# Modulation steps of two and four weight blocks, and a weight ring of seven raw and four split buffers

## The chip, the cores and the metric

The kernel runs on one core of a Trainium2 chip. The metric is the time of one execution on the device, in microseconds (us); a kernel's time is the median of three runs. TensorE (PE in the profile) multiplies, ScalarE (ACT) and VectorE (DVE) prepare operands and empty the accumulators, GpSimd (POOL) helps them, and SyncE (SP) does nothing but issue transfers, one after the other, from its queue.

## The reference, cut to what matters

One decoder layer in float32, for a prompt of 256 tokens and 8 sequences of 4 sampled tokens, so 288 token columns in all. The modulation `mod = silu(c) @ w_ada + b_ada` has 9 rows (one prompt, eight sequences) and 6 x 2048 columns, which are split into shift, scale and gate of two sub-layers.

```
sh1, sc1, gt1, sh2, sc2, gt2 = split(mod, 6)
u   = rms_norm(x) * (1 + sc1) + sh1
mix = token_mixers(u, ...)          # w_in, gated delta rule, causal pooling, w_proj_a/b, w_out
x   = x + gt1 * mix
h   = rms_norm(x) * (1 + sc2) + sh2
x   = x + gt2 * ((silu(gate) * up) @ w_down),   gate, up = split(h @ w_gate_up, 2)
```

The weights, some 360 MB, are read once each. `w_ada` alone is 2048 x 12288 numbers, 100 MB of them.

## The kernel before, in words

**The large products.** `gemm` (line 129) makes a panel of 512 output columns in four accumulators of PSUM. It goes through the contraction in groups of KB = 2 blocks of 128 rows. For each group `load_split` (line 117) loads a raw weight tile of 128 x 1024 float32 (512 KB), and for each of its two blocks ScalarE casts a high half `wh` (line 123) and VectorE, now and then GpSimd, subtracts it to get a low half `wl` (line 124). A group is 24 products on TensorE (line 141): four accumulators, two blocks, and the three terms high x high, high x low, low x high. There are 472 groups: 208 in the mixer (numbers 0 to 207 here, in the order of the program) and 264 in the feed-forward part (208 to 471).

**The buffers.** Raw tiles stand in a ring of RAW = 5, high halves in a ring of WH = 6 and low halves in another of 6, which is three groups of two. A tile is loaded or written when the tile that had its place is no longer needed: a raw tile when its low halves are made, a split tile when TensorE has used it for the last time. A raw tile and two pairs of split tiles take the same room per partition, so that two of the one can be had for two less of each of the other kind.

**The modulation.** `ada` (line 184) computes columns of `mod` straight from raw float32 weights, without a split: four products (eight records in a trace) with the 32-column tile of the conditioning, for each block of 128 rows of `w_ada`. It is a generator. Each step loads the blocks of `pair` steps of the contraction, does their products, and yields. `Fill` advances it between groups of the large products: after each group it adds `every` to a count, and takes a step for each whole number. In the order of the program there are these generators:

- `first_ada`, shift and scale of the first norm, in five pieces (`STEPS`) for 2, 2, 4, 4 and 4 blocks of the hidden size. Each must be done before the first large product with these blocks, since their normed input is scaled by it. Their raw tiles stand in a ring of 4 of their own (pool `st`).
- `later`, gate of the first and scale and shift of the second sub-layer, during the rest of the mixer. Each block of rows takes two raw tiles (`per` = 2), and these stand in the ring of RAW that the large products use.
- `last_ada`, gate of the second sub-layer, from the last of the mixer into the feed-forward part, also in that ring.

**The order.** A scheduler places each engine's instructions beforehand, from the program's order, from priorities and from its own estimate of times; on the chip each engine then works through its list strictly in order, and waits where an operand or a buffer isn't free. SyncE's list holds all loads of weights. At the start of the feed-forward part it also holds a load of the final norm's gain (`fg`, line 1036), whose place is that of tiles that VectorE (line 1028) needs until the second norm is done. The pooling branch loads its own small weights `pw` (line 850) through the same list.

Of the kernel before, what the change touches and what calls it, by code (L numbers as in the profile page):

```python
# [22 lines left out]
H = 8  # L23
DFF = 5632
KB = 2
RAW, WH = 5, 6
NQ = 21
EPS = 1e-6

# [1 line left out]
M_SH1, M_SC1, M_GT1, M_SH2, M_SC2, M_GT2 = 0, 16, 32, 48, 64, 80  # L31
# [42 lines left out]
def tile_step(ctx: ExitStack, tc: tile.TileContext, at, t):  # L74
# [21 lines left out]
    def bc(ap, axis, shape):  # L96
        return ap.unsqueeze(axis).broadcast_to(shape)

    def in_turn(ins):

        tc.stamp_issue_order_token(ins.ins, "modulation")


    def load_raw(srcs, pool=None, kbs=KB):
        n = KB * 512
        if pool is None:
            raw = wpool.tile([P, n], F32, tag="raw", name="raw", bufs=RAW)
        elif pool is qp:
            raw = fquad("raw").rearrange("p k n -> p (k n)")[:, 0:n]
        else:  # L110
            raw = pool.tile([P, n], F32, tag="raw", name="raw", bufs=4)
        raw = raw.rearrange("p (k n) -> p k n", k=kbs)
        for ap, lo, hi in srcs:
            dma(out=raw[:, :, lo:hi], in_=ap.rearrange("(k p) n -> p k n", p=P))  # L114
        return raw
# [11 lines left out]
    def gemm(srcs_of, xs, evac, kbs, eng=vec, late=False):  # L127


        ps = [psg.tile([P, 512], F32, tag="g", name=f"g{j}") for j in range(4)]  # L130
        kbs = list(kbs)
        for c in range(0, len(kbs), KB):
            wh, wl = load_split(srcs_of(kbs[c]), eng)
            for j in range(4):
                o = ps[j][:, 0:N]
                last = c + KB == len(kbs)
                terms = [(w, x, i) for i in range(KB) for w, x in ((wh, 0), (wh, 1), (wl, 0))]
                if late and c == 0:
                    terms.sort(key=lambda v: v[1])
                for n, (w, x, i) in enumerate(terms):  # L140
                    pe.matmul(o, w[i][:, j * P:(j + 1) * P], xs(kbs[c + i])[x], start=c + n == 0,  # L141
                              stop=last and n == 3 * KB - 1)
                if last:
                    with tc.high_priority():
                        evac(j, o)
            fill()

    def cols_of(w, c0):
        return lambda kb: [(w[kb * P:(kb + KB) * P, c0:c0 + 512], 0, 512)]
# [30 lines left out]
    def ada(*d0s, n=16, pool=None):  # L180

        m = n * len(d0s)
        w = m // 4 * P
        ps = psd.tile([P, 512], F32, tag="ada", name="ada")
        per = max(m // 8, 1)
        step = max(8 // m, 1)
        pair = 2 if m == 8 else 1
        for c in range(0, 16, step * pair):
            loads = []
            for k in range(c, c + step * pair, step):  # L190
                raws = []
                for x in range(per):
                    if per > 1:
                        d = (d0s if len(d0s) > 1 else (d0s[0], d0s[0] + 8))[x]
                        srcs = [(t["w_ada"][0, k * P:(k + 1) * P, d * P:(d + 8) * P], 0, 1024)]
                    else:
                        srcs = [(t["w_ada"][0, k * P:(k + step) * P, d0 * P:(d0 + n) * P], i * n * P, (i + 1) * n * P)
                                for i, d0 in enumerate(d0s)]
                    raws.append(load_raw(srcs, qp if pool and d0s[0] == M_SH1 and k >= 8 else pool, step))
                loads.append((k, raws))  # L200

            todo = [(k, raws, i, j) for k, raws in reversed(loads) for i in range(step) for j in (2, 3, 0, 1)]
            for y, (k, raws, i, j) in enumerate(todo):
                x, q = divmod(j, 4 // per)
                with tc.high_priority() if y else nullcontext():
                    in_turn(pe.matmul(ps[32 * j:32 * j + 32, 0:w], cpad[:, k + i, :], raws[x][:, i, q * w:(q + 1) * w],  # L206
                                      start=c == 0 and y < 4, stop=c + step * pair == 16 and y + 4 >= len(todo)))
            if c + step * pair < 16:
                yield
        sb = wpool.tile([P, 512], F32, tag="adasb", name="adasb", bufs=1)  # L210
        act.copy(sb[:, 0:w], ps[:, 0:w])
        for i in range(0, w, P):
            pe.transpose(ps[:, i:i + P], sb[:, i:i + P], ident)
        pv = ps[:, 0:w].rearrange("p (b q m) -> p q b m", q=4, m=32)
        k = 4 // len(d0s)
        for i, d0 in enumerate(d0s):
            md = mod[:, d0:d0 + n, :].rearrange("p (q b) m -> p q b m", q=k)
            v = va[:, d0:d0 + n].rearrange("p (q b) -> p q b", q=k)
            vec.tensor_tensor(md, pv[:, i * k:(i + 1) * k, :, 0:9], bc(v, 3, [P, k, n // k, 9]), ALU.add)
        yield  # L220
# [19 lines left out]
    fill = Fill()  # L240
# [4 lines left out]
    FIRST = (C_Q, C_XP, C_K, C_XP + 512, C_V, C_Z, C_GB, C_GB + 512, C_GB + 1024)  # L245
    STEPS = ((0, 2), (2, 4), (4, 8), (8, 12), (12, 16))
    later = chain(*(ada(d) for d in (M_GT1, M_SC2, M_SH2)))
    last_ada = ada(M_GT2)

    def first_ada(k0, k1, pool):  # L250
        return ada(M_SH1 + k0, M_SC1 + k0, n=k1 - k0, pool=pool)
# [54 lines left out]
    with tc.tile_pool(name="st", bufs=1) as st:  # L306
# [68 lines left out]
        for n, (k0, k1) in enumerate(STEPS):  # L375
            dn = k1 - k0
# [23 lines left out]
            if n == 1:  # L400

                for p in range(2):
                    pst = aux("pst")
                    for h in range(3):
# [3 lines left out]
                        for j in range(4):  # L408
                            m = 24 * (4 * h + j)
# [3 lines left out]

            more = n + 1 < len(STEPS)
            fill.gen = first_ada(*STEPS[n + 1], st) if more else later
            fill.every = 8 / (dn // KB * len(FIRST) - 5) if more else 0.4
            for p, c0 in enumerate(FIRST):
                def evac(j, ps, n=n, p=p):
                    a = acc[p][:, j, :]
# [544 lines left out]
    for p in range(4):  # L964
# [31 lines left out]
            for k in range(3):  # L996
                scaled_samples(k)
        gemm(cols_of(t["w_out"][0], 512 * p), xs_m, evac, range(16))
    fill.gen, fill.every, fill.n = last_ada, 0.15, 5


    rn = cst.tile([P, 3], F32, name="rn")
# [124 lines left out]
```

## Time and profile before

| | |
|---|---|
| median of 3 runs | 1842.74 us (1838.03 to 1844.19) |
| the profiled execution | 1836.14 us, span of its instructions 1834.4 us |
| granted clock of TensorE | 0.991 over the span |
| busy: TensorE, VectorE, ScalarE, GpSimd | 97%, 54%, 41%, 11% |
| read from HBM | 361.16 MB, 201 GB/s over the span |

A row of the page's groups gives line, engine, operation, out<-in by the program's names, and after the bar the busy time, the mean time of one in ns, and the idle time before. Products are pipelined, so the duration of one (some 0.29 us) is longer than the step from one to the next; the steps between starts are what counts. A granted clock of 1.00 is 2.4 GHz and 0.50 is 1.2 GHz, and nothing between occurs in this trace.

### The profile page before, as it was taken

The page shows a single profiled execution, that of the slowest core. Times are in us where ns is not written, and L with a number is a line of the kernel's source. Part 1 is how long each engine was busy: PE and PEld are TensorE (multiplying, and loading weights), DVE is VectorE, ACT ScalarE, POOL GpSimd, SP SyncE. Part 2 cuts the span into 40 slices and gives each one's busy share as a digit, 9 for nine tenths or more (in the row PEclk, how much of TensorE's full clock was granted, in tenths as well). Part 3 has the DMA queues.
Part 4 walks back from the last instruction along what each step waited for, and adds up shares of the span by engine and source line. Part 5 has one row for each costly group of instructions (what it writes and reads, how often), then busy time and mean ns, then how long its engine had stood idle before and what let it go on. Part 6 is the DMA issues. An engine that isn't in the chain of part 4 may idle for free.

```text
span 1834.4 us, 37797 instructions
## 1 busy us (share of the span) xinstructions
PE 1785.7 (97%) x14778; PEld 1657.4 (90%) x14778; DVE 986.2 (54%) x2126; ACT 746.4 (41%) x1522; POOL 206.7 (11%) x376
## 2 busy tenths in 40 slices
PE   5999999999999999999998999999999999999997
PEld 4889998878988787889988999999999999999997
DVE  2466579665645665565555444454444454444454
ACT  4533356433444232344443443443333444444333
POOL 1000025340102232211142000000000000000000
PEclk9999999999999999999999999999999999999999
DMA  9898766666676584876566766655555555555552
GB/s 305 289 322 276 227 204 199 211 213 201 213 244 219 170 253 162 264 255 199 175 217 202 218 198 195 213 181 166 165 168 163 170 163 163 164 169 163 161 160 98
DMA packets 227210, 371.23 MB, mean 202 GB/s; under 512 B 18335, under 2 KB 118168, under 8 KB 226608
## 3 DMA queue, kind: packets, MB, share of 16 engines
q1 hardware_dynamic: 223224, 357.02, 61.0%
q0 software_dynamic: 3808, 11.80, 2.1%
q8 instruction: 116, 1.90, 0.4%
q14 instruction: 62, 0.51, 0.1%
HBM read 361.16 MB, written 7.96 MB: 201 GB/s over the span
## 4 chain that ended last, share of the span: by engine, by line
PE 86%; DMA 6%; DVE 5%; ACT 1%; issue 1%; SPq 0%; POOL 0%; POOLq 0%; ACTq 0%; DVEq 0%
PE g L141 76%; PE ada L206 4%; DMA raw<-in_w_in_dram 3%; DMA raw<-in_w_ada_dram 2%; DVE cy L274 1%; DVE wl L124 1%; PE pss L746 1%; DVE rq L1028 1%; ACT wh L123 1%; PE pks L700 1%; PE py L872 0%; SPq L114 0%; PE py L631 0%; PE pp L636 0%; DMA pw<-in_pool_w_dram 0%
## 5 line engine op out<-in xcount | busy, mean ns | idle before, releaser
L141 PE MATMUL g<-rq,wh 128*128 128x288 f32 x7296 | 1493.2, 299 | 10.3 <-ACT wh L123 4.0
L141 PEld LDWEIGHTS g<-rq,wh 128*128 128x128 f32 x7296 | 1172.9, 188 | 64.4 <-issue 22.7
L141 PE MATMUL g<-rq,wl 128*128 128x288 f32 x3648 | 1075.2, 296 | 0.7 <-POOL wl L124 0.7
L124 DVE TENSOR_TENSOR wl<-raw,wh 128x512 fp32r<-128x512 f32 x910 | 598.8, 692 | 661.4 <-ACT wh L123 659.8
L123 ACT CAST wh<-raw 128x512 fp32r<-128x512 f32 x944 | 543.9, 618 | 878.5 <-PE g L141 630.3
L141 PEld LDWEIGHTS g<-rq,wl 128*128 128x128 f32 x3648 | 687.6, 189 | 7.4 <-issue 4.5
L206 PE MATMUL ada<-raw,cpad 128*32 128x512 f32 (+2 forms) x1152 | 106.6, 473 | 15.3 <-DMA raw<-in_w_ada_dram 14.9
L168 POOL TENSOR_TENSOR ro<-ro,cfix 128x1 f32<-128x1 f32 (+1 forms) x3 | 1.7, 557 | 844.1 <-DVE ro L1091 844.1
L423 DVE TENSOR_TENSOR acc<-acc,g 128x288 f32<-128x288 f32 x144 | 62.2, 449 | 22.7 <-PE g L141 22.4
L206 PEld LDWEIGHTS ada<-raw,cpad 128*32 128x32 f32 x1152 | 28.0, 113 | 39.3 <-issue 19.4
L124 POOL TENSOR_TENSOR wl<-raw,wh 128x512 fp32r<-128x512 f32 x34 | 46.6, 1393 | 45.7 <-ACT wh L123 45.4
L141 PE MATMUL g<-q,wh 128*128 128x288 f32 x256 | 51.0, 294 | 0.0
L274 DVE SCALAR_TENSOR_TENSOR cy<-xc,vb,cy 128x312 f32<-128x312 f32 x72 | 43.6, 623 | 5.3 <-ACT cy L272 4.7
L141 PEld LDWEIGHTS g<-q,wh 128*128 128x128 f32 x256 | 41.3, 189 | 0.0
L141 PE MATMUL g<-q,wl 128*128 128x288 f32 x128 | 37.9, 296 | 0.0
L935 DVE SCALAR_TENSOR_TENSOR x<-g,mod,x 128x256 f32<-128x256 f32 x48 | 23.0, 480 | 12.5 <-PE g L141 11.5
L1061 DVE TENSOR_TENSOR fgg<-fgg,g 128x288 f32<-128x288 f32 x44 | 20.0, 454 | 10.9 <-PE g L141 8.7
L141 PEld LDWEIGHTS g<-q,wl 128*128 128x128 f32 x128 | 24.0, 188 | 0.0
L749 DVE SCALAR_TENSOR_TENSOR sst<-sst,cds,pss 128x128 f32<-128x128 f32 x64 | 18.1, 343 | 7.9 <-PE pss L746 7.7
L1056 DVE SCALAR_TENSOR_TENSOR fgg<-fth,fgg 128x288 f32<-128x288 f32 x44 | 20.0, 455 | 3.9 <-ACT fgg L1055 1.3
L1054 ACT ACTIVATE fth<-g 128x288 f32<-128x288 f32 x44 | 18.1, 412 | 7.3 <-PE g L141 5.4
L644 POOL MEMSET T<- 32x64 f32 x8 | 1.1, 142 | 168.5 <-PE pab L432 151.0
(324 smaller groups left out, 948.4 us busy)
## 6 DMA issues: line engine op xcount, KB each, us to landing
raw<-in_w_gate_up_dram SPq DMA_DIRECT2D x352, 256.0 KB, 3.1
raw<-in_w_in_dram SPq DMA_DIRECT2D x144, 512.0 KB, 5.3
raw<-in_w_ada_dram SPq DMA_DIRECT2D x128, 512.0 KB, 4.4
raw<-in_w_down_dram SPq DMA_DIRECT2D x88, 512.0 KB, 3.8
raw<-in_w_ada_dram SPq DMA_DIRECT2D x128, 256.0 KB, 5.5
raw<-in_w_out_dram SPq DMA_DIRECT2D x32, 512.0 KB, 3.7
raw<-in_w_proj_b_dram SPq DMA_DIRECT2D x16, 512.0 KB, 4.6
raw<-in_w_proj_a_dram SPq DMA_DIRECT2D x16, 512.0 KB, 5.0
```

What stands on the lines that cost most here:

```text
L123: act.copy(wh[i], raw[:, i, :])
L124: eng.tensor_tensor(wl[i], raw[:, i, :], wh[i].bitcast(F32), ALU.subtract)
L141: pe.matmul(o, w[i][:, j * P:(j + 1) * P], xs(kbs[c + i])[x], start=c + n == 0, stop=last and n == 3 * KB - 1)
L206: in_turn(pe.matmul(ps[32 * j:32 * j + 32, 0:w], cpad[:, k + i, :], raws[x][:, i, q * w:(q + 1) * w], start=c == 0 and y < 4, stop=c + ste ...
L274: vec.scalar_tensor_tensor(y[:, 0:L], xc[:, m:m + L], vb[:, 24 * m + no:24 * m + no + 1], y[:, 0:L], ALU.mult, ALU.add)
L423: vec.tensor_tensor(a, a, ps, ALU.add)
L700: pe.matmul(pks[NS * i:NS * i + NS, x * P:(x + 1) * P], km[i // 2][:, i % 2, b, :], S[i][:, b, :], start=b == 0, stop=b == NB - 1)
L746: pe.matmul(pss, kt[r, 0, :], wx[b0 // 4][r].rearrange("p b v -> p (b v)"), start=True, stop=True)
L935: vec.scalar_tensor_tensor(x[:, j, 0:NP], ps[:, 0:NP], mod[:, gate + d, 0:1], x[:, j, 0:NP], ALU.mult, ALU.add)
L1028: vec.scalar_tensor_tensor(b[:, d, 0:NP], hp, mod[:, M_SH2 + k, 0:1], a[:, d, 0:NP].bitcast(F32), ALU.add, ALU.subtract)
L1056: vec.scalar_tensor_tensor(gg, th, 1.0, gg, ALU.add, ALU.mult)
L1061: vec.tensor_tensor(gg, gg, ps, ALU.mult)
```

## The change

Two constants and three rates change. RAW goes from 5 to 7 and WH from 6 to 4. `pair` is now chosen by `m`, the number of output blocks: the pieces with 4 blocks in shift and scale each (m = 8) take four blocks of rows at a time instead of two, the full-width ones of `later` and `last_ada` (m = 16) two instead of one, and the second piece with 2 (m = 4) two steps instead of one; the very first piece stays as it was. `every` is halved, or nearly so, to go with it.

```
-RAW, WH = 5, 6
+RAW, WH = 7, 4
...
-        pair = 2 if m == 8 else 1
+        pair = {4: 1 if d0s[0] == M_SH1 else 2, 8: 4, 16: 2}[m]
...
-            fill.every = 8 / (dn // KB * len(FIRST) - 5) if more else 0.4
+            fill.every = 4 / (dn // KB * len(FIRST) - 5) if more else 0.2
...
-    fill.gen, fill.every, fill.n = last_ada, 0.15, 5
+    fill.gen, fill.every, fill.n = last_ada, 0.08, 2
```

In the built order TensorE stops for the modulation (a run of line 206 between other instructions) at 96 places before and at 52 now. Three places follow.

TensorE, end of the second and start of the third piece's panels (`g_1309` to `g_1312` are the accumulators of group 17, `g_1362` to `g_1365` those of group 18; line 213 turns the finished modulation for group 18's input). Before:

```order
L141 MATMUL g_1311<-rq,wl 128x288
L206 MATMUL ada<-raw,cpad 32x256 x8
L141 MATMUL g_1312<-rq,wh 128x288 x2
L141 MATMUL g_1312<-rq,wl 128x288
L141 MATMUL g_1312<-rq,wh 128x288 x2
L141 MATMUL g_1312<-rq,wl 128x288
L432 MATMUL pab<-xn_271,wab 32x288 x4
L141 MATMUL g_1362<-rq,wh 128x288
L141 MATMUL g_1363<-rq,wh 128x288
L141 MATMUL g_1364<-rq,wh 128x288
L206 MATMUL ada<-raw,cpad 32x256 x8
```

And now:

```order
L213 MATMUL ada<-cfix,adasb 128x128 x2
L141 MATMUL g_1311<-rq,wl 128x288
L141 MATMUL g_1312<-rq,wh 128x288 x2
L141 MATMUL g_1312<-rq,wl 128x288
L141 MATMUL g_1312<-rq,wh 128x288 x2
L141 MATMUL g_1312<-rq,wl 128x288
L206 MATMUL ada<-raw,cpad 32x256 x16
L432 MATMUL pab<-xn_271,wab 32x288 x4
L141 MATMUL g_1362<-rq,wh 128x288
L141 MATMUL g_1363<-rq,wh 128x288
```

Line 213 has moved up to seven products ahead of group 18's start; before it stood 43 products ahead. The stop behind it is the fourth piece's first, with four blocks instead of two. Only 30 products lie between it and the last stop of the third piece, which uses the same four raw tiles.

SyncE, start of the feed-forward part (each `raw` row of `w_gate_up` is one group's weights, in two halves). Before:

```order
L114 DMA raw_12348<-in_w_gate_up_dram 128x2x256 x2
L114 DMA raw_12383<-in_w_gate_up_dram 128x2x256 x2
L114 DMA raw_12418<-in_w_ada_dram 128x1024
L114 DMA raw_12420<-in_w_ada_dram 128x1024
L1036 DMA fg_12110<-in_final_g_dram 128x2048
L114 DMA raw_12426<-in_w_gate_up_dram 128x2x256 x2
```

And now:

```order
L114 DMA raw_12375<-in_w_gate_up_dram 128x2x256 x2
L114 DMA raw_12410<-in_w_gate_up_dram 128x2x256 x2
L114 DMA raw_12465<-in_w_gate_up_dram 128x2x256 x2
L114 DMA raw_12500<-in_w_gate_up_dram 128x2x256 x2
L114 DMA raw_12535<-in_w_gate_up_dram 128x2x256
L1036 DMA fg_12110<-in_final_g_dram 128x2048
```

Before, groups 209 to 214 and two blocks of the modulation stand ahead of `fg`, and group 215 (`raw_12426`) behind it; now groups up to 217 and a half of 218 stand ahead of it.

TensorE, a group in the middle of a panel of `w_down` (accumulators `g_15564` to `g_15567`), which stands for most of the second half. Before:

```order
L141 MATMUL g_15564<-rq,wh 128x288 x2
L141 MATMUL g_15564<-rq,wl 128x288
L141 MATMUL g_15565<-rq,wh 128x288 x2
L141 MATMUL g_15565<-rq,wl 128x288
L141 MATMUL g_15566<-rq,wh 128x288 x2
```

And now:

```order
L141 MATMUL g_15564<-rq,wh 128x288 x2
L141 MATMUL g_15565<-rq,wh 128x288
L141 MATMUL g_15564<-rq,wl 128x288
L141 MATMUL g_15564<-rq,wh 128x288 x2
L141 MATMUL g_15565<-rq,wh 128x288
```

A product with the high half of the next accumulator now stands ahead of the first one with a low half.

## Rows read from the trace of the kernel before

**Rows 1.** Page: the chain that ended last, shares by engine.

```profile
PE 86%; DMA 6%; DVE 5%; ACT 1%; issue 1%; SPq 0%; POOL 0%; POOLq 0%; ACTq 0%; DVEq 0%
```

**Rows 2.** Page, costliest groups: products, and the two halves of a split.

```profile
L141 PE MATMUL g<-rq,wh 128*128 128x288 f32 x7296 | 1493.2, 299 | 10.3 <-ACT wh L123 4.0
...
L124 DVE TENSOR_TENSOR wl<-raw,wh 128x512 fp32r<-128x512 f32 x910 | 598.8, 692 | 661.4 <-ACT wh L123 659.8
L123 ACT CAST wh<-raw 128x512 fp32r<-128x512 f32 x944 | 543.9, 618 | 878.5 <-PE g L141 630.3
```

**Rows 3.** Chain in order of time: start us, us, what.

```profile
114.87 5.22 DMA raw<-in_w_ada_dram
...
378.92 6.74 DMA pw<-in_pool_w_dram
...
1210.81 501.87 PE g L141 x3768
```

**Rows 4.** Stretches: A:B length, busy PE PEld DVE ACT POOL, PEclk, DMA share, GB/s.

```profile
100.00:125.00 25.00, 24.57 (x224) 20.13 (x223) 17.41 (x39) 8.38 (x14) 0.00 (x0) 1.00 0.94 326
275.00:300.00 25.00, 23.74 (x180) 20.78 (x179) 23.35 (x54) 16.95 (x45) 16.26 (x35) 1.00 0.63 198
375.00:400.00 25.00, 21.92 (x159) 16.97 (x158) 15.60 (x48) 9.35 (x29) 10.13 (x16) 0.86 0.72 228
525.00:550.00 25.00, 23.58 (x177) 20.74 (x170) 14.72 (x32) 10.65 (x27) 3.92 (x16) 1.00 0.81 253
979.80:986.60 6.80, 6.12 (x25) 5.74 (x25) 4.81 (x8) 4.73 (x11) 2.27 (x2) 0.50 0.53 159
```

**Rows 5.** TensorE in order of time (start us, us, ...): one block, two blocks.

```profile
1005.54 0.29 PE L141 MATMUL g<-rq,wl 128*128 128x288 f32 x1
1005.77 1.06 PE L206 MATMUL ada<-raw,cpad 128*32 128x512 f32 x8
1006.76 0.53 PE L141 MATMUL g<-rq,wh 128*128 128x288 f32 x2
...
817.36 0.29 PE L141 MATMUL g<-rq,wl 128*128 128x288 f32 x1
817.58 1.92 PE L206 MATMUL ada<-raw,cpad 128*32 128x512 f32 x16
819.43 0.53 PE L141 MATMUL g<-rq,wh 128*128 128x288 f32 x2
```

**Rows 6.** TensorE in order of time, groups 214 to 215.

```profile
974.53 1.06 PE L206 MATMUL ada<-raw,cpad 128*32 128x512 f32 x8
979.54 0.67 PE L141 MATMUL g<-rq,wh 128*128 128x288 f32 x2 [3.95 <-ACT wh L123]
```

**Rows 7.** SyncE in order of time, same place.

```profile
960.28 3.22 SPq L114 DMA_DIRECT2D raw<-in_w_ada_dram  x2
972.07 0.33 SPq L1036 DMA_DIRECT2D fg<-in_final_g_dram  x1
972.49 13.69 SPq L114 DMA_DIRECT2D raw<-in_w_gate_up_dram  x14
```

**Rows 8.** SyncE in order of time, fourth piece: two blocks, four transfers.

```profile
113.53 1.76 SPq L114 DMA_DIRECT2D raw<-in_w_ada_dram  x4
```

**Rows 9.** TensorE and ScalarE in order of time, ahead of group 18.

```profile
109.98 0.38 PE L213 MATMUL ada<-cfix,adasb 128*128 128x128 f32 x2
...
115.89 1.15 ACT L395 CAST rq<-xn 128x1152 fp32r<-128x1152 f32 x1 [2.35 <-DVE xn L392]
```

**Rows 10.** ScalarE, VectorE, TensorE in order of time: split and start of group 223.

```profile
1002.14 1.14 ACT L123 CAST wh<-raw 128x512 fp32r<-128x512 f32 x2 [2.06 <-PE g L141]
...
1002.79 1.30 DVE L124 TENSOR_TENSOR wl<-raw,wh 128x512 fp32r<-128x512 f32 x2 [1.90 <-ACT wh L123]
...
1010.05 0.43 PE L141 MATMUL g<-rq,wh 128*128 128x288 f32 x2
```

## The prediction

> **What bounds the kernel now.** I began with the chain that ended last: TensorE has 86% of it, transfers 6%, VectorE 5% [rows 1]. So the question at each place is how densely TensorE is fed. Then the chain in order of time: from 1210.81 us on it is one piece of 3768 products in 501.87 us, 133.2 ns each [rows 3], so a group of 24 takes 3.20 us and nothing waits there. What can be won lies in the modulation's stops, in the few holes of the first 1000 us, and in nothing else. Then the views by stretch, for these holes [rows 4], and the order of time around each. The groups of the page show why TensorE is seldom short of weights: ScalarE spends 630 us waiting for TensorE to give a split buffer back, and VectorE 660 us waiting for ScalarE [rows 2]. The splits run ahead until buffers end; WH is what limits them.
>
> **A. Fewer stops: -10.3 us.** A stop for one block runs from the product that starts at 1005.54 to the next at 1006.76, 1.22 us, where two products would lie 0.13 apart: it costs 1.09. A stop for two runs from 817.36 to 819.43, 2.07 us, and costs 1.94 [rows 5]. Joining two stops saves 2 x 1.09 - 1.94 = 0.24 us: the product in flight is drained once, not twice. The narrower stops weren't paired like this in the rows; I give them the same. The built order has 96 stops before and 52 after, so 44 x 0.235 = 10.3. All of it is on the path, as TensorE is. The work itself doesn't shrink.
>
> **B. The load behind `fg`: -6.5 us.** At 974.53 TensorE does a stop of 1.06 us and then stands for 3.95 us until 979.54 [rows 6], short of group 215's weights. SyncE's list shows why: `fg` could go only at 972.07, 11.8 us after the issue before it began at 960.28, and group 215's load stands behind it, issued at 972.49 [rows 7]. After the hole the clock is at its lower level: 0.50 between 979.80 and 986.60, where 25 products were done in 6.8 us instead of 25 x 0.133 = 3.3 [rows 4], a loss of 3.5, some of it a late low half. Now groups 215 to 217 stand ahead of `fg`, and 218, behind it, is needed three groups or 9.6 us later. So 3.95 + 3.5 = 7.4 go. Against it, two stops of two blocks (1.92 each, [rows 5]) now stand ahead of the second norm's broadcast, where the last buffer of the second is given back only by the first; I charge one block, 1 us. What is late next is GpSimd's subtraction, which paces the panel; if it takes the wait's place, 3 of the 6.5 stay and no more is lost. Ends: -7.5 and -3.
>
> **C. Four blocks at once in the early pieces: +7.5 us.** The private ring holds four raw tiles. Before, a stop used two, while the other two were loading. Now a stop uses all four, and no transfer for the next can start until it is over. Two blocks take from their first issue at 113.53 [rows 8] to the landing at 114.87 + 5.22 = 120.09 [rows 3], 6.56 us. Two more are 1.05 MB; at 326 GB/s, the rate of this stretch with the transfer engines 94% busy [rows 4], 3.2 us more, so at most 9.8 us; 6.56 if they hide in its latency; I take 8.0, about the middle. What covers it is the products between two stops of the built order. In the third and fourth pieces they are 60, 66, 66, 30, 48, 60 and 84, at 133 ns: 8.0, 8.8, 8.8, 4.0, 6.4, 8.0 and 11.2 us, with smaller products beside the first (24 transposes), the fourth (0.4 us) and the fifth (0.7). So two stops wait: 8.0 - 4.4 = 3.6 and 8.0 - 7.1 = 0.9. The 3.6 is nearly the hole of B, which was followed by half clock; I add 3.0, which is 7.5. The same place has a second reason to wait: the third piece's modulation is ready only seven products and a stop ahead of group 18, while before it took from 109.98 until 115.89 + 1.15 = 117.04, 7.1 us, from line 213 to the cast input [rows 9]; that runs beside the wait for the transfer and adds little. Behind the waiting stop everything on TensorE is queued, and VectorE's sums with it. Ends: at 6.56 us one wait of 2.2 and no drop of the clock, +2.2; at 9.8 us 5.4 + 2.7 + 1.8 + 1.0 + 1.0 = 11.9, and two drops, +18.
> The Trainium skill, page "DMA: Bandwidth & Descriptors", section "Anatomy of one DMA", gives a fit of some 2.0 us fixed and bytes over 436 GB/s, for another issuing path. By it four blocks (2.1 MB) would take an estimated 6.8 us, C would be +2.4 and the sum -15.4. The rows disagree: two blocks would take 4.4 by it and took 6.56.
>
> **D. The pooling hole: -3 us.** Between 375 and 400 us TensorE is idle for 3.1 us, and the clock's mean is 0.86 [rows 4], so 7 us at half, a loss of 3.5. The hole is a `pw` load that took 6.74 us from its issue at 378.92 [rows 3]. In the new order large products stand between the pooling's products, and the last `pw` still goes behind a group's load, so I take half of the 6.6. Ends: -6.6 if all of it closes, +2 if the wait returns larger.
>
> **E. Two split groups instead of three: +3 us.** Group 223's cast began at 1002.14, its last low half was ready at 1002.79 + 1.30 = 1004.09, and its first product began at 1010.05 [rows 10]: 6.0 us ahead. With one pair less the cast starts one group later, 3.2 us, which leaves 2.8. So the feed-forward part pays nothing: 264 groups x 0. But where VectorE is full (23.35 of 25 us between 275 and 300 [rows 4]) its low halves come late already, and the buffers smooth that. There are nine panels in the fifth piece; at best none waits, at worst each waits half a group's time, 14 us (all of it only if VectorE had no idle time left). TensorE there still idles only 1.3 us in 25, so I take a value near the lower end, 3. Ends: 0 and 14.
>
> **F. The raw ring: -1 us.** Between 525 and 550 TensorE idles 1.4 us [rows 4], with loads of `w_in` on the chain. With seven raw tiles the loads of products are less often behind a tile of the modulation: -2. In return a step in the shared ring needs four tiles, and where its last takes the place of a group just split it may come late: +1. Ends: -4 and +5.
>
> **Sum.** -10.3 - 6.5 + 7.5 - 3 + 3 - 1 = -10.3 us. The profiled execution took 1836.14 us, of which 1834.4 are the span; it would take 1825.8. The median shown, 1842.74, is 6.6 above that execution, so I forecast 1842.74 - 10.3 = 1832.4 us.
>
> **Rival 1, the early stops starve (about 1843).** C at its upper end, +18 instead of +7.5: net 0. For it: the transfer engines are 94% busy there, and loads of `w_in` for two more raw tiles now stand ahead of the modulation's in SyncE's list. Against: those loads would be needed anyway. It decides from a landing time of some 9 us on.
> The Trainium skill, page "TensorE: Matmul & The Clock Gate", section "HAM oscillation — how this bites in real kernels", says that a kernel that waits for a transfer in each round can pay the return to full clock in each. By it rival 1 would cost 3 us more at each such wait; the trace has it after the 3.95 us hole, while the stretch from 100 to 125, with 0.4 us of idling, stays at 1.00 [rows 4].
>
> **Rival 2, the splits are late (about 1859, slower).** The new order puts a high product of the next accumulator ahead of the first low one in most groups of the second half, which is what a scheduler does that expects low halves to be late. If it is right by 0.1 us in each of the 264 feed-forward groups, that is +26, net +16. Against it: the 2.8 us just worked out; it decides only once the split's 1.95 us (1002.14 to 1004.09) grow beyond 4.7.
>
> **Rival 3, all covers hold (about 1822).** C at +2.2 and D at -6.6, E at 0: -22 from the same parts, taken as 1822. For it: the scheduler placed each stop where its own estimate had the data.
>
> **Numbers.** The likeliest case has 0.45, rival 1 0.21, rival 2 0.13, rival 3 0.16, something else 0.05. About 0.3%, 5.5 us, is what a measurement of this kernel can tell from no change. The likeliest case (own range 1825 to 1839) is faster by more than that in 0.38 of its 0.45; with rival 3 and a share of the rest, faster has 0.56. Same has 0.07 from it and 0.14 from rival 1 and some of the rest, 0.23. Slower has 0.07 from rival 1's own upper side, rival 2 and the rest, 0.21. The range reaches from rival 3's far side to just above rival 1: 1819 to 1850.
>
> **What would show it.** A: 52 runs of line 206, the two-block ones about 2.07 us from product to product. B: no idle before group 215, and no half clock near 980. C: waits of line 206 for `w_ada` near 110 to 130 us, the largest at the fourth piece's first stop. D: less than 3 us idle near 380. E: products of line 141 waiting for ScalarE or VectorE between 230 and 330, none after 1000. I am wrong if the second half's products lie more than 133 ns apart, or if the early waits together pass 12 us.

## The result: faster, by more than twice the forecast

The changed kernel takes 1816.49 us (median of 4 runs, 1814.67 to 1817.97), the kernel before, timed beside it, 1840.38 us (4 runs, 1834.8 to 1844.19). The ratio is 0.9873, 95% interval 0.9845 to 0.9900: some 24 us less. The forecast was 1832.4 us, 10 us less, with a range that ended at 1819. The sign was right, the size was not. The two profiled executions differ by 21.5 us (1836.14 and 1814.67 us).

### The profile after

Page of the changed kernel: the chain that ended last, shares by engine, which answers to [rows 1].

```profile
PE 93%; DMA 3%; DVE 2%; issue 1%; ACT 1%; POOL 0%; SPq 0%; POOLq 0%; ACTq 0%; DVEq 0%
```

Transfers fell from 6% to 3% of the chain and VectorE from 5% to 2%. So most of what went is waiting, not only stops. The costliest groups of its page, which answer to [rows 2]:

```profile
L141 PE MATMUL g<-rq,wh 128*128 128x288 f32 x7296 | 1441.7, 298 | 10.6 <-DVE acc L423 6.1
...
L123 ACT CAST wh<-raw 128x512 fp32r<-128x512 f32 x944 | 544.6, 618 | 842.9 <-PE g L141 766.1
```

The cast is idle for about as long as before (842.9 us, before 878.5), but it now waits for TensorE in 766 of it; before, in 630. What was waited for in the other 248 us of before is what the forecast didn't ask. The stretches of the changed kernel that answer to [rows 4], with the place ahead of the feed-forward part where the clock is low now as the last (A:B, length, busy PE PEld DVE ACT POOL, PEclk, DMA share, GB/s):

```profile
100.00:125.00 25.00, 21.23 (x181) 17.40 (x180) 14.10 (x33) 7.11 (x12) 0.00 (x0) 0.86 0.89 303
275.00:300.00 25.00, 20.62 (x146) 18.81 (x147) 23.75 (x51) 13.70 (x35) 15.34 (x28) 0.93 0.55 164
375.00:400.00 25.00, 25.00 (x217) 21.75 (x220) 12.30 (x27) 11.21 (x25) 4.33 (x7) 1.00 0.79 254
525.00:550.00 25.00, 25.00 (x194) 23.40 (x193) 13.27 (x26) 11.38 (x22) 0.94 (x5) 1.00 0.67 211
930.00:945.00 15.00, 9.72 (x55) 6.64 (x56) 6.94 (x18) 5.89 (x15) 8.54 (x14) 0.77 0.96 314
```

The first two are worse than before (a wait near 116 us, one near 284), and the last is new. The third and fourth have no idle time left, where before had 3.1 and 1.4 us.

To see where the time went, I read the start of every group from the trace: the records of line 141 in order, laid beside the built order, which names the split buffer of each. The columns are the forecast's terms, with A shared out by the stops that each stretch lost (15, 5, 10 + 2 + 5, 3, 4), and the time that the changed kernel gained (-) or lost against the profiled execution of before. Each kernel has one profile: five that have the rings and steps of before up to group 54, before among them, reach that group between 253.6 and 257.7 us, so a row of less than some 4 us says little.

| groups | forecast | measured |
|---|---|---|
| start to 54 | A -3.5, C +7.5: +4.0 | +0.7 |
| 54 to 80 (fifth piece, next panel) | A -1.2, D -3, E +3: -1.2 | -11.2 |
| 80 to 204 (rest of the mixer) | A -4.0, F -1: -5.0 | -3.0 |
| 204 to 216 | A -0.7, B -6.5: -7.2 | -4.8 |
| 216 to the last group | A -0.9 | -2.9 |
| sum | -10.3 | -21.2 |

Ten of the missing eleven us lie between groups 54 and 80, where D and E were. The row is a loss of 10.6 us up to group 72 and a gain of 21.8 between 72 and 80.

### The profile page after: what moved, and what is told of

It reads as the page before. It is cut to its first block, busy times and chain, and to the rows that moved or that the text cites. A ratio compares the mean times of both kernels' runs of the same rounds, so it can differ in the third digit from the quotient of the medians.

```text
span 1812.9 us, 37810 instructions
## 1 busy us (share of the span) xinstructions
PE 1762.6 (97%) x14778; PEld 1652.5 (91%) x14778; DVE 985.5 (54%) x2126; ACT 748.3 (41%) x1522; POOL 207.6 (11%) x376
## 4 chain that ended last, share of the span: by engine, by line
PE 93%; DMA 3%; DVE 2%; issue 1%; ACT 1%; POOL 0%; SPq 0%; POOLq 0%; ACTq 0%; DVEq 0%
PE g L141 82%; PE ada L206 5%; DMA raw<-in_w_ada_dram 2%; PE pss L746 1%; DMA raw<-in_w_in_dram 0%; PE pks L700 0%; DVE cy L274 0%; DVE wl L124 0%; PE pnr L533 0%; PE py L631 0%; PE pp L636 0%; PE py L872 0%; DMA pw<-in_pool_w_dram 0%; PE px L973 0%; DMA xt<-in_x_prompt_dram 0%
## 5 line engine op out<-in xcount | busy, mean ns | idle before, releaser
L141 PE MATMUL g<-rq,wh 128*128 128x288 f32 x7296 | 1441.7, 298 | 10.6 <-DVE acc L423 6.1
L141 PEld LDWEIGHTS g<-rq,wh 128*128 128x128 f32 x7296 | 1149.7, 188 | 49.6 <-issue 22.5
L141 PE MATMUL g<-rq,wl 128*128 128x288 f32 x3648 | 1014.2, 296 | 0.3 <-POOL wl L124 0.3
L123 ACT CAST wh<-raw 128x512 fp32r<-128x512 f32 x944 | 544.6, 618 | 842.9 <-PE g L141 766.1
L141 PEld LDWEIGHTS g<-rq,wl 128*128 128x128 f32 x3648 | 664.7, 188 | 4.2 <-issue 1.7
L206 PE MATMUL ada<-raw,cpad 128*32 128x512 f32 (+2 forms) x1152 | 100.7, 483 | 18.4 <-DMA raw<-in_w_ada_dram 18.3
L206 PEld LDWEIGHTS ada<-raw,cpad 128*32 128x32 f32 x1152 | 33.7, 117 | 55.9 <-issue 39.4
L1056 DVE SCALAR_TENSOR_TENSOR fgg<-fth,fgg 128x288 f32<-128x288 f32 x44 | 20.0, 455 | 12.4 <-ACT fgg L1055 12.1
```

Source lines behind the costliest of these rows:

```text
L123: act.copy(wh[i], raw[:, i, :])
L1056: vec.scalar_tensor_tensor(gg, th, 1.0, gg, ALU.add, ALU.mult)
```

## The experiments

Each kernel ran with before on the same chip; "before" had medians of 1837.7 to 1843.2 there. The rings are written as (raw tiles, split buffers of each kind): (5, 6) before, (7, 4) changed. "Old steps" are the modulation's `pair` and rates of before, "new steps" those of the change. Differences of 2 or 3 us between kernels of different batches aren't read, as before itself moved by more.

### Which part of the change?

**Rings alone**, in the kernel before:

```
-RAW, WH = 5, 6
+RAW, WH = 7, 4
```

> The rings alone: seven raw tiles and four split buffers of each kind (two groups) with the modulation as before, one or two blocks at a stop; 90 stops in the built order. Theory 1 (the part of the gain that the forecast missed, some 13 us, lies in the mixer's loads: more raw tiles take the raw waits and the pooling hole away): 1840 - 6 x 0.24 - 12 = about 1827. Theory 2 (the gain is that of the modulation's steps): within 3 us of before, 1837 to 1843. The forecast's own terms E and F: +3 - 1 - 1.4, so about 1841. Rival 2's mechanism (two split groups are too few): slower, 1850 or more.

1827.82 us, ratio 0.9937 (0.9917 to 0.9958): -12.5. Theory 1 had 1827. D, E and F had -1 together.

**Steps alone**, the changed kernel with the rings of before:

```
-RAW, WH = 7, 4
+RAW, WH = 5, 6
```

> The modulation's new steps alone, 52 stops, with five raw tiles and six split buffers as before. Theory 1: it keeps A (-10.3), C and part of B, but a step of the shared ring needs four of five raw tiles, so the loads of products come later and the holes of the mixer stay or grow: 1833 to 1845. Theory 2: nearly the whole gain, 1815 to 1822. A third theory (rings and steps are only good together: the four raw tiles of a step starve the split with five) has it slower than before, 1845 or more, with waits of line 141 for the raw loads in the second half of the mixer.

1833.25 us, 0.9959 (0.9940 to 0.9979): -7. A, B and C had -9.3. Theory 2 falls. So does the third theory in its form "slower", though its reason shows up below.

**Early and late steps.** In the changed kernel, one of the two as before:

```
-        pair = {4: 1 if d0s[0] == M_SH1 else 2, 8: 4, 16: 2}[m]
+        pair = {4: 1, 8: 2, 16: 2}[m]
```

(the early ones, with 8 for 4 in their rate) or

```
+        pair = {4: 1 if d0s[0] == M_SH1 else 2, 8: 4, 16: 1}[m]
```

(the late ones, with 0.4 for 0.2, and 0.15 and 5 for 0.08 and 2).

> The changed kernel with the early pieces as before (one block in the second piece, two in the third to fifth), the late steps and the rings as changed; 64 stops, 12 more than the changed kernel. If C (+7.5, or about +5 by the trace after) is right: 1816.5 - 5 + 12 x 0.24 = 1814 (1812 by the forecast's C). If the early change costs nothing net and the order of the fifth piece matters: 1816 to 1821. In the trace the wait of 3.8 us at 112 us and the half clock behind it should be gone.

1817.23 us, 0.9880 (0.9855 to 0.9905): no difference from the changed kernel that can be told. The wait at 112 us and its half clock are gone, and 12 stops are back. So C costs about what its stops save, 12 x 0.235 = 2.8 us, give or take the 2.5 of the interval, and not 7.5.

> The changed kernel with the late modulation as before (one block at a stop, every 2.5 groups), the early pieces and the rings as changed; 78 stops, 26 more than the changed kernel. Theory 2 with A alone: 1816.5 + 26 x 0.24 = 1822.7. With B given back as well (fewer groups issued ahead of the final gain's load, the hole of 4 us and half clock): 1828. Theory 1 (rings carry the rest): not above 1829. If the late steps carry the missed part: 1830 to 1838.

1826.43 us, 0.9935 (0.9912 to 0.9957): 10 us slower than the changed kernel, more than the 26 stops (6.1), in the range of A with a part of B. At the rings (7, 4) the late steps carry nearly the whole gain of the steps.

### Which part of the rings?

**Six and five; five and four.** Old steps:

```
-RAW, WH = 5, 6
+RAW, WH = 6, 5
```

and, in the other kernel,

```
+RAW, WH = 5, 4
```

> The step between the two rings: six raw tiles and five split buffers of each kind, modulation as before. Theory 1a (each raw tile more takes a part of the mixer's load waits): halfway between before and the rings alone, about 1834. Theory 3 (any other size of the rings makes the scheduler put large products between the pooling's and the chunks' small products; that order, not the ring, is the gain): as much as the rings alone, 1825 to 1830.

> Fewer split buffers alone: four of each kind, five raw tiles, modulation as before. The forecast's E says +3, 1843. Theory 1a: slower than before, 1840 to 1845, since the raw tiles that bring the gain are missing. Theory 3: it gains nearly as much as the rings alone, 1826 to 1832, since its built order has the pooling's products among the large ones too; the stretch from group 72 to 80 should be some 20 us shorter than before, the one from 54 to 72 some 7 us longer.

1819.90 us, 0.9879 (0.9859 to 0.9899), and 1831.72 us, 0.9941 (0.9921 to 0.9961). Fewer split buffers alone gain 10 us. E had them as a loss. The two raw tiles more of the rings alone add 3.9 us by the medians and less than 1 by the ratios to before. And (6, 5) with old steps is within 4 us of the whole change. Both speak for theory 3, the order, against 1a.

**Split buffers alone by one pair; the rate alone; less of both.** Old steps; one line each in three kernels:

```
+RAW, WH = 5, 5
...
+            fill.every = 8 / (dn // KB * len(FIRST) - 5) if more else 0.38
...
+RAW, WH = 4, 5
```

> One split buffer of each kind less and nothing else: five raw tiles, five split buffers, modulation as before, 98 stops. The forecast's E: +1 to +3, 1843. Theory 3b (with three whole split groups the scheduler lets the splits run ahead and leaves the pooling's and the chunks' work late, so that up to 45 small products stand in one row before group 80; with fewer than six the longest row is 22): 1820 to 1830. If the sixth raw tile is what the ring of six and five gains from: 1836 to 1843.

> The kernel before with the late modulation at 0.38 steps a group instead of 0.4; the rings as before; its built order has a row of 86 small products before group 80, where before has 45. Theory 3a (before just has an unlucky order, and any disturbance of it gains): 1825 to 1832. Theory 3b (three whole split groups make the row): no gain, 1838 to 1850, and the stretch from group 72 to 80 as long as before or longer.

> Less of both than before: four raw tiles and five split buffers of each kind, modulation as before; the longest row of small products in groups 54 to 84 is 21. If buffers are what the mixer lacks (theory 1): slower than before, 1845 or more. Theory 3b: faster than before in groups 54 to 80 by some 10 us all the same; with a raw tile less the loads of products come later, which may cost up to 5 in the mixer and more in the feed-forward part, where each group's load then has one raw tile less to run ahead in: 1828 to 1838.

1836.32 us, 0.9985 (0.9965 to 1.0005); 1839.77 us, 1.0003 (0.9984 to 1.0022); 1859.50 us, 1.0101 (1.0073 to 1.0129). The first and the last miss what theory 3b said of the time, and the second speaks against 3a: this disturbance of the order gains nothing. By the starts of groups 3b is half right. At group 80 the kernel (5, 5) is 16.3 us ahead of before, and (4, 5) still 3.4; then (5, 5) loses 14.8 us up to group 204, and (4, 5) 29.3. The sixth raw tile alone makes 1836.3 into 1819.9. So buffers do count, behind group 80, and theory 1a was dropped too early.

**Two split groups in the fifth piece only.** Rings and steps of before; the six split buffers are four and two under two names, and groups 54 to 79 use the four alone. With that held off, each engine's built order is that of before.

```
+        x, nb = ("x", 2) if next(turn["n"]) % 3 == 2 and not turn["two"] else ("", 4)
```

> The kernel before (five raw tiles, six split buffers, steps as before), with the splits of groups 54 to 79 held to four of the six buffers of each kind; elsewhere the ring turns over three groups as before. Theory 3b (the third split group lets splits run ahead of the pooling's and the chunks' work there): the longest row of small products is 20 instead of 45; groups 72 to 80 shorter by 15 to 21 us, 54 to 72 longer by 5 to 12, net at group 80 about -10; if the later groups keep it, 1830; if five raw tiles give it back as they did with five split buffers, 1836 to 1840, with the loss after group 80. Rival (the gain at 72 to 80 comes from the raw tiles or from the steps): no change up to group 80, 1838 to 1844.

1843.38 us, 1.0015 (0.9995 to 1.0035). Up to group 80 it does what 3b says: 12.4 us are lost between 54 and 72, 21.4 are gained between 72 and 80, and it stands 9.0 us further ahead than at group 54. The rival falls. The built order shows the reason: the longest row of small products without a large one between (pooling, chunks) is 45 before and 20 here and in the changed kernel. Then 24.7 us are given back up to group 204 (in a profiled execution of 1849.9 us, 6.5 above the kernel's median, with a granted clock of 0.86 between 550 and 600 us, where before has 1.00). The gain exists, and this kernel doesn't keep it.

That raw tiles decide whether it is kept shows in all the profiles together. Group 204 starts between 926.6 and 942.9 us in the nine kernels with five raw tiles, before among them, at 954.1 with four, and between 914.0 and 920.2 in the ten with six or seven, whatever their split buffers and steps. Before is dense between groups 80 and 204 (its TensorE waits 3.6 us there), but begins late; the kernels with five raw tiles that reach group 80 earlier lose it.

**New steps with few raw tiles.** The changed kernel with (5, 4); with (6, 4); and the kernel before with (6, 4):

```
+RAW, WH = 5, 4
...
+RAW, WH = 6, 4
...
+RAW, WH = 6, 4
```

> The changed kernel with five raw tiles instead of seven; 52 stops. If the two raw tiles more are what the four-tile steps of the late modulation live on: slower than the changed kernel by 10 to 15 us between groups 128 and 176, 1826 to 1835. If the raw tiles do little (the forecast's F, -1): 1815 to 1819.

> The changed kernel with six raw tiles instead of seven, four split buffers of each kind. If raw tiles are the supply: between five (1843.4) and seven (1816.5), 1822 to 1835, with ScalarE's casts waiting 20 to 50 us for loads between 400 and 960 us. If the built order decides by accident: anywhere, and the casts' waits don't go with the time.

> The same with the modulation's steps as before. With the old steps five raw tiles made 1831.7 and seven 1827.8; if raw tiles are the supply, 1826 to 1832, since a step of two raw tiles leaves four or five for the products. The new steps' gain, which is +12 (a loss) at five raw tiles and -11 at seven, should then be about 0 at six: within 6 us of the kernel beside it.

1843.43 us, 1.0018 (1.0001 to 1.0035); 1814.21 us, 0.9850 (0.9824 to 0.9877); 1820.20 us, 0.9883 (0.9858 to 0.9908). The first is 27 us slower than the changed kernel, twice what was expected. With six, both are faster than expected and the gain is all there: not the steady dose that I expected, but a step between five and six. A step of two blocks needs four raw tiles at once; of five, that leaves one for the products. That this is why the new steps lose at (5, 4) is likely, but not isolated. At (5, 6) the same steps gain 7 us. And by the profiles of the two (5, 4) kernels the new steps lose 10.0 us between groups 54 and 80 and 7.6 behind 216, but 0.9 between 80 and 204, where most steps with four tiles stand.

| split buffers, steps | 4 raw | 5 raw | 6 raw | 7 raw |
|---|---|---|---|---|
| 6, old / new | | 1840 / 1833.3 | | |
| 5, old / new | 1859.5 / - | 1836.3 / - | 1819.9 / 1819.0 | |
| 4, old / new | | 1831.7 / 1843.4 | 1820.2 / 1814.2 | 1827.8 / 1816.5 |

A seventh raw tile gains nothing: with the old steps it costs 7.6 us, and why wasn't tried.

### What a raw tile too few does

ScalarE's casts in the mixer, one row a kernel (between 400 and 960 us: busy time, mean ns, then the idle time ahead of them and what ended it). Before, (5, 6) with old steps:

```profile
L123 ACT CAST wh<-raw 128x512 fp32r<-128x512 f32 x257 | 148.5, 618 | 266.6 <-PE g L141 138.6 <-DMA raw<-in_w_in_dram 71.4 <-DMA raw<-in_w_proj_a_dram 19.8
```

(5, 5) with old steps, then (6, 5):

```profile
L123 ACT CAST wh<-raw 128x512 fp32r<-128x512 f32 x251 | 147.3, 618 | 269.4 <-PE g L141 168.5 <-DMA raw<-in_w_in_dram 69.7 <-DMA raw<-in_w_proj_b_dram 13.6
```

```profile
L123 ACT CAST wh<-raw 128x512 fp32r<-128x512 f32 x257 | 151.4, 618 | 256.4 <-PE g L141 227.8 <-DMA raw<-in_w_in_dram 15.2 <-DMA raw<-in_w_proj_a_dram 5.3
```

The changed kernel with (5, 4), then as it is, (7, 4):

```profile
L123 ACT CAST wh<-raw 128x512 fp32r<-128x512 f32 x252 | 145.7, 618 | 271.7 <-PE g L141 150.9 <-DMA raw<-in_w_in_dram 62.1 <-DMA raw<-in_w_proj_a_dram 20.9
```

```profile
L123 ACT CAST wh<-raw 128x512 fp32r<-128x512 f32 x259 | 149.7, 618 | 251.3 <-PE g L141 220.7 <-issue 21.5 <-DMA raw<-in_w_gate_up_dram 6.0
```

In these rows the casts with five raw tiles wait 83 to 91 us for loads, with six or seven 6 to 21. (5, 4) with old steps, the fastest of five raw tiles, has 22.7 there. The kernels with six or seven all take 1814 to 1828 us, those with five 1832 to 1843; among those with six or seven the waits don't order the times. Nor is a cast's wait a wait of TensorE: before has those 91 us, and its TensorE waits for 3.6 us between groups 80 and 204. TensorE seldom waits for a cast itself. What it waits for stands behind the cast. ScalarE and TensorE of before in order of time (start us, us, ..., idle before and its releaser):

```profile
531.84 1.14 ACT L123 CAST wh<-raw 128x512 fp32r<-128x512 f32 x2 [2.69 <-DMA raw<-in_w_in_dram]
...
533.15 0.19 ACT L267 COPY xc<-g 128x32 f32<-128x32 f32 x1
...
533.39 0.54 PE L141 MATMUL g<-rq,wh 128*128 128x288 f32 x2 [1.42 <-ACT xc L267]
```

Lines 266 and 267 empty an accumulator. They stand behind a cast that waits 2.69 us for its load, and TensorE stands for 1.42 us, since it can't begin the next products until the accumulator is empty. The changed kernel with (5, 4), the chain through its longest wait after 300 us (start us, us, what):

```profile
376.90 10.15 DMA raw<-in_w_proj_b_dram
...
387.13 0.63 ACT wh L123
...
388.39 0.68 DVE wl L124
...
389.10 0.31 DVE Y L669
...
389.54 0.66 PE pp L672 x4
```

A raw tile of `w_proj_b` is late, its cast waits on ScalarE, its low halves wait for the cast on VectorE, and the copy of line 669, which has nothing to do with that tile, stands behind them: TensorE waits 5.6 us for the copy. The next two waits of that kernel over 1 us, 2.5 us at 610 and 2.0 at 781 us, have chains of the same kind, and the clock is at its lower level for 6.8, 3.4 and 3.4 us at these three places. The kernel with (7, 4) has no wait of over 1 us and no lower clock between 300 and 930 us. That is how a late load that is needed only later stops TensorE now. The Trainium skill, page "PSUM — Partial Sum Buffer", section "Engine vs sequencer instructions", calls the queues of ScalarE, VectorE and GpSimd strictly first in, first out; the rows agree. It isn't the only way in which a late load costs: with (5, 4) and old steps TensorE's longest wait between 400 and 940 us (2.6) is that of the modulation's own products for a raw tile. How much of the 27 us goes by either way wasn't summed.

### Two terms by themselves, and a better kernel

**The gain's load, and the pooling's loads, from GpSimd's queue**, in before; two kernels:

```
-    dma(out=fg, in_=t["final_g"].unsqueeze(0).broadcast_to([P, DM]))
+    dmg(out=fg, in_=t["final_g"].unsqueeze(0).broadcast_to([P, DM]))
...
-                dma(out=pw, in_=t["pool_w"][0, g].rearrange("(i p) d -> p i d", p=P))
+                dmg(out=pw, in_=t["pool_w"][0, g].rearrange("(i p) d -> p i d", p=P))
```

> The kernel before with the final gain's load issued by GpSimd, so that no group's load stands behind it. It measures B alone: 3.95 us of hole and 3.5 us of half clock should go, -7.4, so about 1833. If GpSimd's subtraction then paces the panel: about 1836. If the same hole opens for another reason: 1839 to 1841. GpSimd's issue waits for VectorE as SyncE's did, ahead of the subtractions of that panel: a loss if these come late.

> The kernel before with the pooling's weights loaded from GpSimd's queue, so that they don't stand behind a group's load; the built order near the pooling stays nearly that of before. It measures D by the queue alone: -6.6 at most, about 1834. Theory 3 (the load is not what makes the stretch long, the chain of small products without large ones between them is): -1 to -4, 1836 to 1840, with TensorE still waiting near 380 us, for ScalarE or VectorE then.

1833.10 us, 0.9955 (0.9936 to 0.9975), and 1838.67 us, 0.9980 (0.9964 to 0.9996). B was -7.4 for this form. Its median says -8.7 (by the interval, -4.6 to -11.8), the trace -6.0 between groups 204 and 216: B holds. D by its queue is worth 3 (0.7 to 6.6 by the interval), and by the trace 0.9 between groups 54 and 80. TensorE of before shows why, in order of time:

```profile
381.14 1.07 PE L206 MATMUL ada<-raw,cpad 128*32 128x512 f32 x8 [2.08 <-DMA raw<-in_w_ada_dram]
...
385.70 2.29 PE L872 MATMUL py<-yp,pw 128*128 128x288 f32 x4 [0.48 <-DMA pw<-in_pool_w_dram]
```

Of the 3.1 us of idling there, the pooling's load ended 0.48. The longest part ended with a block of the modulation, in the ring of raw tiles. In the kernel with the load moved, TensorE still waits 1.4 us for such a block.

**Six and five with new steps; the last steps without a head start**, once with (7, 4) and once with (6, 5); all three in the changed kernel:

```
+RAW, WH = 6, 5
...
-    fill.gen, fill.every, fill.n = last_ada, 0.08, 2
+    fill.gen, fill.every, fill.n = last_ada, 0.105, 0
```

> The changed kernel with six raw tiles and five split buffers of each kind instead of seven and four; 52 stops. If the steps' gain (A, 44 x 0.24 = 10.3, of which the late steps showed all and the early ones nothing net) adds to that of the rings six and five (1819.9 with the old steps): 1820 - 6 to 1820 - 10, about 1811, faster than both kernels. If a step of four raw tiles starves a ring of six, or the rings' gain and the steps' are partly the same holes: 1815 to 1819, no better than the changed kernel.

> The changed kernel with the last modulation starting at once but without a head start: 0.105 steps a group from 0, where it had 0.08 from 2; its first step comes eight groups into the feed-forward part and not ahead of the second norm's broadcast. If the two steps there cost what the trace shows between groups 204 and 208 (+3.7, with a wait of 2.28 us for a transfer and 3.5 us of half clock): 1816.5 - 3.7 = about 1813, faster than both kernels. If the hole of B only comes back behind the final gain's load, which now stands nearer: 1816 to 1819.

> The same with six raw tiles and five split buffers. That ring lost 4.8 us between groups 204 and 208 with the steps as changed: 1819 - 4.8 = about 1814. If the hole of B comes back: 1818 to 1821.

1818.98 us, 0.9879 (0.9851 to 0.9906); 1818.69 us, 0.9891 (0.9866 to 0.9915); 1816.78 us, 0.9875 (0.9851 to 0.9898). None beats the changed kernel. In the second the wait for the transfer ahead of the feed-forward part is gone. TensorE then waits for the second norm. Its waits between 920 and 1000 us (waited for: us in total, times, longest):

```profile
PE pn L948 <- DVE sq L987: 3.7, 1, 3.7
```

The two stops had stood beside that norm. The only kernel with a lower median than the changed one is (6, 4) with new steps, 1814.2 against 1816.5; the runs overlap (1811.7 to 1817.1, and 1814.7 to 1818.0), so the two can't be told apart. It does the same with one raw tile less, so with 4 KB per partition less. (A raw tile takes the room of one high and one low half, so that 7 and 4, 6 and 5, and 5 and 6 take the same.)

## Why the prediction was wrong, by its own steps

**A, fewer stops (-10.3): right.** 52 stops, and over all stops of a kind the medians from product to product are 1.22 us for one block and 2.08 for two: 0.23 saved for each pair joined, four 256-column blocks too. The two-block row of the changed kernel ahead of the feed-forward part is one of them:

```profile
927.43 1.92 PE L206 MATMUL ada<-raw,cpad 128*32 128x512 f32 x16
929.28 2.17 PE L948 MATMUL pn<-onec,sq 128*128 128x1 f32 x18
933.73 3.55 PE L206 MATMUL ada<-raw,cpad 128*32 128x512 f32 x16 [2.28 <-DMA raw<-in_w_ada_dram]
```

**B (-6.5): right, with a price that was put too low (1 us).** TensorE no longer waits ahead of group 215, and the clock is 1.00 there (965 to 972 us), where it was 0.50. But the second stop of those rows waits 2.28 us for its transfer and runs at half clock. 4.8 us are left.

**C (+7.5): the first wait as said, the sum too high.** From the first issue at 106.65 to the last landing at 115.94 us four blocks took 9.3 us, near the upper end. Only one stop waits:

```profile
116.08 3.64 PE L206 MATMUL ada<-raw,cpad 128*32 128x256 f32 x32 [3.77 <-DMA raw<-in_w_ada_dram]
```

It is the first stop of the fourth piece, as forecast (line 213, which ends the third piece's modulation, ran at 110.98), and its price is as forecast, too: 3.8 us, and some 3 more with the clock at 0.51 from 114.4 to 121.3 us (the forecast had 3.6 and 3.0). The second wait, of 0.9 us, didn't come. But with A's stops the changed kernel is only 0.7 us behind before at group 54, where 4.0 were forecast, and against the early-old kernel the new early steps neither gain nor lose. So C was too high by some 3 us, no more than the profiles differ among themselves there; where they came from is open.

**D (-3): about right, by a wrong reading.** The waits near 380 us have nearly closed (0.9 us for the pooling's load, 0.3 for a block of the modulation). But the prediction put the whole hole down to the pooling's load, which ended 0.48 us of it; most of it was a wait in the raw ring, which is F's subject.

**E (+3): the first step that failed, by its sign.** Alone, the step from six split buffers to four took 10 us off (1841.8 to 1831.7). Line 141 does wait for VectorE in the fifth piece:

```profile
PE g L141 <- DVE acc L423: 6.1, 5, 4.4
...
PE g L141 <- POOL wl L124: 0.3, 1, 0.3
```

(the changed kernel's waits between 225 and 335 us). It waits for VectorE's sums of the panels, not for low halves, as E had it. None comes after 1000 us, as forecast. But E took split buffers only as a store that TensorE runs down. They are also what lets ScalarE and VectorE run ahead with splits in the scheduler's order, past the pooling's and the chunks' work. With two groups that work comes earlier, which costs 10.6 us between 54 and 72 and gives 21.8 between 72 and 80. The two-in-fifth kernel shows the cause of this part: it changes nothing else up to group 80. That the long row of small products is itself what costs, and no other trait of that order, is likely but not isolated.

**F, "the raw ring: -1 us", ends -4 and +5: the second step that failed, by its size.** Together the rings are worth -12.5 us with old steps and -16.8 with new ones, where D, E and F had -1; that is about what was missed. At four split buffers the two raw tiles are worth 3.9 us with the old steps (1831.7 to 1827.8), at the end of the range, the first of them alone 11.5 (1831.7 to 1820.2), and both 26.9 with the new ones (1843.4 to 1816.5), far outside. Without them E would have been +10 (1833.3 to 1843.4), and the change no gain at all. The error began earlier, in the sentence that WH "is what limits" the splits. It rested on one row over the whole span [rows 2], where TensorE ended 630 of 878 us of the cast's waits; the part after 960 us holds 388 of those 630. The row from 400 to 960 us, above, has 91 of 267 us ended by loads. In before itself that row costs TensorE little; by the starts of group 204 it is the kernels that reach group 80 earlier that lack the raw tiles. And the terms aren't a sum: with four split buffers the new steps are worth +12, -6 and -11 us at five, six and seven raw tiles, with (5, 6) -7 and with (6, 5) -1, while A was one number for all.

**The rivals.** Rival 1 asked whether four tiles at once starve, but of the private ring, which cost what the likeliest case had for its first wait. In the shared ring the new steps lose 12 us at (5, 4), which rival 1 didn't ask. Rival 2 falls, since the second half's products stay at 133 ns: 3720 in 493.87 us. In the changed kernel's chain:

```profile
1197.91 493.87 PE g L141 x3720
```

Rival 3 was nearest in time (1822; its own terms add up to 1820.5), but not for its own reasons: C's first wait did come, with its drop of the clock, D by itself is worth 3, and E is no zero but a gain.

## What to carry to other kernels

Ask of each ring what its waits end in stage by stage; a row over the whole span answers for the longest stage only. A late load can cost where its consumer stands in an in-order queue, long before the data is needed, so look at what is queued behind the waiting instruction. When work is batched to save a fixed cost, count the buffers that a batch holds at once against those that the main stream needs meanwhile: here, with four split buffers, six raw tiles keep the gain and five turn it into a loss.

## What the runs showed that I had not expected

Two split groups were better than three in the fifth piece, by 9 us at group 80 with nothing else changed. And the kernel before spreads over 15 us (1833.7 to 1849), as do most kernels with four or five raw tiles (8 to 18 us; (5, 4) with old steps 3), while those with six or seven spread over 3 to 9. One profile gives a hint: the kernel with the gain's load moved has a clock of 0.73 between 550 and 575 us, where before has 1.00 in the same order of work. Whether such stretches make the spread wasn't tried.
